# Gate projections with 512 moving columns and one PSUM bank per token block, and one address modulo 512 bytes for all float32r operands

## The chip, the core and the metric

The kernel runs on one core of a Trainium2 chip. A core has a matrix engine (PE, with its weight loads shown as PEld), a vector engine (DVE), an activation engine (ACT), a general engine (POOL) and a queue engine (SP) that issues DMAs. Each takes its own instructions in program order and waits for the others at semaphores. SBUF is the working memory (128 partitions), PSUM the memory that matmuls write to: eight banks of 512 float32 values per partition. The metric is the device time of one execution in microseconds (us); less is better.

## What is computed

One decoder block on 512 tokens of width 1024:

```python
u = rmsnorm(h, norm1_g)
proj = einsum("bsd,de->bse", u, w_in)
(g_qkv, g_z, g_a, g_b, d_q, d_k, d_v, i_q, i_k, i_w, gate_a, gate_b) = split(proj)
...   # gated delta rule on g_qkv, g_a, g_b: o_gdn (8 heads of 128)
o_gdn = rmsnorm(o_gdn, gdn_norm_g) * silu(z)
...   # top-128 sparse attention on d_q, d_k, d_v with the indexer: o_dsa (8 heads of 128)
mixed = sigmoid(gate_a + gb[:D]) * o_gdn + sigmoid(gate_b + gb[D:]) * o_dsa
h = h + mixed @ w_out
hn = rmsnorm(h, norm2_g)
...   # ConvGLU: up 1024 -> 2 x 2816, causal conv of width 3, SiLU gate, down
out = rmsnorm(h, final_g)
```

The change lies in the three projections `g_z`, `gate_a` and `gate_b`, 3 x 1024 columns of `w_in`.

## The kernel before

**Splitting.** Every float32 matrix product is made of three float32r matmuls (`passes`): an operand is split into a rounded part `hi` and a rest `lo`, and `lo*hi`, `hi*lo` and `hi*hi` are added in PSUM. Weights come packed as pieces of 128 x 1024. `piece` loads one into `raw`; ACT rounds it into `whi`, POOL or DVE subtracts it into `wlo`. There are three buffers of each. The normalised tokens stand transposed and split in `uTh`/`uTl`, later in `hTh`/`hTl`.

**Stages, in order of the code.** (1) Input, its norm, the indexer's and the `dv` projections. (2) `gdn_half(0)`: projections of four heads (`channel_major`: weights stationary, 512 tokens moving), convolution and SiLU on DVE and ACT, sums of squares (`kqt`), decay matrices `ge`, Gram matrices (`kk`, into `MT` and `at`), `vt`; then a triangular inverse: blocks of `MT` go through DRAM (`bl`, `nn`) to a loop of 30 pairs of DVE instructions (`tw`, `wi`), back through DRAM into `MT`, then small matmuls (`m`); then a recurrence over four chunks of tokens (`kS`, `TR`, `upd`, `o`). (3) The top-k of the indexer, the `dk` and `dq` projections. (4) `gdn_half(1)`, the same for the other four heads. (5) Attention, 32 items of head and token block (`lg` scores, `pe` softmax, `pT` transposes, `oB`). (6) The gate projections: `token_major` makes 256 columns for 512 tokens, with tokens stationary and weights moving; `z_chunk`, `ga_chunk` and `gb_chunk` apply the results to `at` and `oB`; `mix_chunk` adds both branches and transposes them (`mixT`). (7) Out-projection, (8) up-projection with the ConvGLU, (9) down-projection and the final norm.

**What sets the order.** A scheduler with a timeline of its own merges the stages when the program is built, and fixes a static order of instructions on each engine. Tiles come from pools. A tile with a `tag` takes the next of `bufs` buffers of that tag in the order of the code, and its first writer waits for the last reader of the tile that had the buffer before. PSUM has eight banks under four tags: `acc` 3, `tp` 2, `pT` 1, `rec` 2. All of `kqt`, `kk`, `vt`, `m`, `kS`, `TR`, `upd` and `o` take their bank from `rec`; scores (`lg`) and `mixT` from `tp`; projections from `acc`.

**Places.** A buffer's address follows from the sizes of what was allocated before it. In the built program `whi`, `wlo`, the first tiles of x (`xgh`, `xgl`), `mix` and the first eight `act` tiles begin at byte 448 modulo 512; `uTh`, `uTl`, `hTh` and `hTl` at 128; the other fourteen `act` tiles at 480.

Of the kernel before, what the change touches and what calls it, by code (L numbers as in the profile page):

```python
# [9 lines left out]
F = mybir.dt.float32  # L10
R = mybir.dt.float32r
I32 = mybir.dt.int32
AF = mybir.ActivationFunctionType
OP = mybir.AluOpType
# [7 lines left out]
KT = D // 128  # L22
# [12 lines left out]
    0, 3072, 4096, 4104, 4112, 5136, 5392, 5648, 6160, 6224, 6232, 7256)  # L35


_GATES = [("z", 0), ("z", 1), ("ga", 0), ("ga", 1), ("gb", 0), ("gb", 1), ("gb", 2), ("gb", 3),
          ("z", 2), ("z", 3), ("ga", 2), ("ga", 3)]


def _in_chunks():

    t = []
    t.append(("dv", [_DV, _DV + 128]))
    t.append(("small", None))
    t += [("iq", [_IQ + 256 * j, _IQ + 256 * j + 128]) for j in range(2)]
    gdn = [[("gdn", [_QKV + 1024 * part + 512 * hh + 256 * j + 128 * i for i in range(2)])
            for part in (1, 0, 2) for j in range(2)] for hh in range(2)]
    dsa = [("dk", [_DKV, _DKV + 128])]  # L50
    dsa += [("dq", [_DQ + 256 * j, _DQ + 256 * j + 128]) for j in range(4)]
    t += gdn[0] + dsa + gdn[1]
    off = {"z": _Z, "ga": _GA, "gb": _GB}
    t += [(k, [off[k] + 256 * j, off[k] + 256 * j + 128]) for k, j in _GATES]
    return t


def _pack_weights(w_in, w_out, w_up, w_down):

    out = []  # L60

    def chunk(w, starts):
        c = np.concatenate([w[:, s:s + 128] for s in starts], axis=1)
        c = c.reshape(2, 4, 128, 256).transpose(0, 2, 1, 3).reshape(2, 128, 1024)
        out.extend([c[0], c[1]])

    for kind, starts in _in_chunks():
        if kind == "small":
            c = np.zeros((D, 128), w_in.dtype)
            c[:, 0:64] = w_in[:, _IK:_IK + 64]  # L70
# [12 lines left out]
    return np.ascontiguousarray(np.stack(out))
# [3 lines left out]
def hybrid_block(ctx: ExitStack, tc: tile.TileContext, x: bass.AP, xc: bass.AP, wp: bass.AP,  # L87
                 chan: bass.AP, rows: bass.AP, out: bass.AP):
    nc = tc.nc
    V, A, P, T = nc.vector, nc.scalar, nc.gpsimd, nc.tensor  # L90

    const = ctx.enter_context(tc.tile_pool(name="const", bufs=1))
# [3 lines left out]
    def acc(name="acc"):  # L96
        return psum.tile([128, 512], F, name=name, tag="acc", bufs=3)
# [93 lines left out]
    def piece(lo_engine):  # L191
        raw, hi, lo = load()
        A.copy(hi, raw)  # L193
        lo_engine.tensor_sub(lo, raw, hi.bitcast(F))  # L194
        return hi, lo

    def passes(o, lhs, rhs, first, last, shared=False):


        (lh, ll), (rh, rl) = lhs, rhs  # L200
        a = T.matmul(o, lh, rl, start=first, stop=False, skip_group_check=shared)  # L201
        T.matmul(o, ll, rh, start=False, stop=False, skip_group_check=shared)  # L202
        return a, T.matmul(o, lh, rh, start=False, stop=last, skip_group_check=shared)  # L203

    def cols(pc, k, n, c0, c1):
        return tuple(w.rearrange("p (k c) -> p k c", c=n)[:, k, c0:c1] for w in pc)

    uTh = const.tile([128, KT, S], R, name="uTh", tag="uTh")
    uTl = const.tile([128, KT, S], R, name="uTl", tag="uTl")

# [56 lines left out]
    for tb in range(NT):  # L267
# [3 lines left out]
        _, root = rms_of(ss, out=r4[:, tb:tb + 1])  # L271
# [15 lines left out]
    def u_blk(k, tb):  # L287
        return uTh[:, k, 128 * tb:128 * tb + 128], uTl[:, k, 128 * tb:128 * tb + 128]

    def token_major(eng):  # L290

        pcs = [piece(eng), piece(eng)]
        ps = [acc().rearrange("p (t c) -> p t c", c=256) for _ in range(2)]
        for i in range(2):
            for tb in range(NT):
                for k in range(4):
                    kk = 4 * i + k
                    passes(ps[tb // 2][:, tb % 2], u_blk(kk, tb), cols(pcs[i], k, 256, 0, 256),
                           kk == 0 and tb % 2 == 0, kk == KT - 1, shared=True)
        return ps  # L300

    def channel_major(eng, src=None, second=P):
# [61 lines left out]
    def sc8(name):  # L364
        return const.tile([128, NT, H], F, name=name)
# [1 line left out]
    def b8(ap):  # L367
        return ap.unsqueeze(1).to_broadcast([128, NT, H])

    beta, gd, G, GL, eG, neG, kde, dl = (sc8(n) for n in ("beta", "gd", "G", "GL", "eG", "neG", "kde", "dl"))  # L370
    s0, s1, s2 = sc8("s0"), sc8("s1"), sc8("s2")
    A.activation(beta, sm[:, :, 72:80], AF.Tanh, scale=0.5)
    V.tensor_scalar(beta, beta, 0.5, 0.5, op0=OP.mult, op1=OP.add)
    na = const.tile([128, H], F, name="na")
# [25 lines left out]
    A.activation(dl, GL, AF.Exp)  # L400
    V.tensor_sub(kde, GL, G)
    A.activation(kde, kde, AF.Exp)
    nG = sc8("nG")
    V.tensor_scalar(nG, G, -1.0, None, op0=OP.mult)
    gt = tp("gt")
    T.transpose(gt[0:32, 0:128], G.rearrange("p t h -> p (t h)"), ident)
# [29 lines left out]
    for b in range(1, NT):  # L436
        n = 128 * (b + 1)
        score[b] = mask[:, m_off[b]:m_off[b] + n]
        for h in range(H):
            p = tp("rel")[:, :n]  # L440
# [309 lines left out]
    mix = [[big(FL, "mix") for _ in range(2)] for _ in range(4)]  # L750

    def gate_bias(off):
        gb = PR.tile([128, 256], F, name="gbias", bufs=2)
        A.dma_start(gb, bcast(2048 + off, 256))
        return gb.unsqueeze(1).to_broadcast([128, 2, 256])

    def tmp(name):
        return PR.tile([128, 512], F, name=name, tag="t", bufs=5).rearrange("p (t c) -> p t c", c=256)

    def gated(o, p, bias):  # L760
        t = tmp("tg")
        V.tensor_add(t, p, bias)
        A.activation(t, t, AF.Tanh, scale=0.5)
        V.scalar_tensor_tensor(o, t, 1.0, o, op0=OP.add, op1=OP.mult)

    def z_chunk(j):
        for t2, p in enumerate(token_major(P)):
            t = tmp("tz")
            A.activation(t, p, AF.Tanh, scale=0.5)
            V.scalar_tensor_tensor(t, t, 1.0, p, op0=OP.add, op1=OP.mult)  # L770
            o = oAv[j][:, 2 * t2:2 * t2 + 2]
            P.tensor_mul(o, o, t)

    def ga_chunk(j):
        bias = gate_bias(256 * j)
        for t2, p in enumerate(token_major(P)):
            gated(oAv[j][:, 2 * t2:2 * t2 + 2], p, bias)

    def gb_chunk(j):
        bias = gate_bias(1024 + 256 * j)  # L780
        for t2, p in enumerate(token_major(P)):
            tb = slice(2 * t2, 2 * t2 + 2)
            t = tmp("tg")
            V.tensor_add(t, p, bias)
            A.activation(t, t, AF.Tanh, scale=0.5)
            for i in range(2):
                o = oB[2 * j + i][:, tb]
                V.scalar_tensor_tensor(o, t[:, :, 128 * i:128 * i + 128], 1.0, o, op0=OP.add, op1=OP.mult)

    def mix_chunk(j):  # L790
        for t2 in range(2):
            tb = slice(2 * t2, 2 * t2 + 2)
            pm = tp("mixT").rearrange("p (i t d) -> p i t d", i=2, t=2)
            for i in range(2):
                o = oB[2 * j + i][:, tb]
                V.tensor_add(o, o, oAv[j][:, tb, 128 * i:128 * i + 128])
                for t in range(2):
                    T.transpose(pm[:, i, t], o[:, t], ident)
            ts = slice(256 * t2, 256 * t2 + 256)
            pmv = pm.rearrange("p i t d -> p i (t d)")  # L800
            A.copy(mix[j][0][:, :, ts], pmv)
            V.tensor_sub(mix[j][1][:, :, ts], pmv, mix[j][0][:, :, ts].bitcast(F))

    oAv = [oA[j // 2].rearrange("p t h d -> p t (h d)")[:, :, 256 * (j % 2):256 * (j % 2) + 256] for j in range(4)]
    for kind, j in _GATES:
        {"z": z_chunk, "ga": ga_chunk, "gb": gb_chunk}[kind](j)
        if kind == "gb" and j < 2:
            mix_chunk(j)
        if kind == "ga" and j >= 2:
            mix_chunk(j)  # L810


    hTh = const.tile([128, KT, S], R, name="hTh", tag="uTh")
# [2 lines left out]
    for q in range(2):  # L816
        nc.sync.dma_start(g2b[q], bcast(1024 + 512 * q, 512))
    ss2 = const.tile([128, NT, 4], F, name="ss2")
    load_sqrt(oAv[3][:, 3, 255:256])
    sp2, hns, hg = [], [], []  # L820
    done = None

# [108 lines left out]


    gf = FR.tile([128, D], F, name="gf")
    A.dma_start(gf, bcast(4 * 1024, D))
    sp3 = []
    load_sqrt(act[-1][:, 0, 511:512].bitcast(F))
# [99 lines left out]
```

## Time and profile before

| | us |
|---|---|
| median of 3 runs (lowest, highest) | 971.64 (965.71, 971.94) |
| the profiled execution's own time | 968.83 |
| its span (first to last instruction) | 966.8 |
| PE / DVE / ACT / POOL busy in the span | 932.6 / 614.6 / 439.8 / 206.6 |

The span is what the trace covers; 2.0 us of the execution lie around it. "Busy" of PE joins records that overlap: a matmul's record lasts until its modelled end, long after the next one has begun. What a matmul costs in a dense stretch is therefore the distance from its start to the next start, not its duration.

### The profile page before, as it was taken

To read this page: it belongs to the slowest core of one execution; us is meant where nothing else is said; L and a number is where in the kernel's file an instruction comes from. 1 tells how busy PE (TensorE), PEld (TensorE's weight loads), DVE (VectorE), ACT (ScalarE), POOL (GpSimd) and SP (SyncE) were. 2 spreads that over 40 slices of the span, in tenths; PEclk is the share of its full clock that TensorE was granted. 3 is DMA by queue.
4 is the path that set the end of the run, shared out by engine and by line. 5 is a ranking of instruction groups with operands and counts; after the bars stand their busy time and mean duration, and the time that the engine had idled before them with its cause. 6 is when DMAs were issued, how large, how long until landed. Compare 5 with 4: busy or idle time off the path is not lost.

```text
span 966.8 us, 14652 instructions
## 1 busy us (share of the span) xinstructions
PE 932.6 (96%) x5671; PEld 804.8 (83%) x5671; DVE 614.6 (64%) x1262; ACT 439.8 (45%) x938; POOL 206.6 (21%) x120
## 2 busy tenths in 40 slices
PE   8979999998999998899999999999999999999997
PEld 8768887876887898799999999888888888888886
DVE  5997999997548949754634546655555665522424
ACT  7446674422458762345444435443444443422213
POOL 3734244521201363211343032000000000000201
PEclk9989999997999999999999999999999999999999
DMA  8222222423211131411322222323222323232222
GB/s 326 88 87 87 88 82 72 120 88 88 88 44 44 46 98 66 99 51 50 137 94 93 83 87 89 109 92 104 87 87 97 101 88 105 90 105 92 87 66 87
DMA packets 39541, 89.29 MB, mean 92 GB/s; under 512 B 15632, under 2 KB 16944, under 8 KB 39472
## 3 DMA queue, kind: packets, MB, share of 16 engines
q1 hardware_dynamic: 24048, 82.05, 26.0%
q10 hardware_dynamic: 15424, 6.31, 2.7%
q8 instruction: 44, 0.72, 0.3%
q14 instruction: 25, 0.20, 0.1%
HBM read 85.18 MB, written 3.16 MB: 91 GB/s over the span
## 4 chain that ended last, share of the span: by engine, by line
PE 69%; DVE 23%; DMA 3%; ACT 2%; issue 1%; POOL 1%; ACTq 0%; SPq 0%; DVEq 0%; POOLq 0%
PE acc L201 17%; PE acc L203 17%; PE acc L202 17%; DVE wi L583 3%; PE d L202 3%; PE d L203 3%; PE d L201 3%; DVE mask L687 2%; DVE y L458 2%; DVE top L686 2%; DVE tw L581 2%; PE lg L726 1%; PE lg L708 1%; DVE uv L415 1%; DVE mask L448 1%
## 5 line engine op out<-in xcount | busy, mean ns | idle before, releaser
L193 ACT CAST whi<-raw 128x1024 fp32r<-128x1024 f32 x136 | 142.2, 1046 | 184.9 <-PE acc L203 83.0
L194 POOL TENSOR_TENSOR wlo<-raw,whi 128x1024 fp32r<-128x1024 f32 x60 | 148.8, 2481 | 291.6 <-ACT whi L193 240.1
L194 DVE TENSOR_TENSOR wlo<-raw,whi 128x1024 fp32r<-128x1024 f32 x76 | 94.2, 1240 | 153.5 <-ACT whi L193 153.3
L202 PE MATMUL acc<-hTh,wlo 128*128 128x512 f32 (+1 forms) x368 | 141.7, 385 | 0.0
L201 PE MATMUL acc<-hTl,whi 128*128 128x512 f32 (+1 forms) x368 | 141.1, 386 | 0.2 <-DVE hTl L835 0.2
L203 PE MATMUL acc<-hTh,whi 128*128 128x512 f32 (+1 forms) x368 | 140.8, 385 | 0.0
L201 PE MATMUL acc<-uTl,whi 128*128 128x512 f32 x272 | 110.9, 409 | 6.1 <-DVE iqf L423 5.5
L202 PE MATMUL acc<-uTh,wlo 128*128 128x512 f32 x272 | 110.6, 407 | 1.6 <-DVE wlo L194 1.6
L203 PE MATMUL acc<-whi,uTh 128*128 128x256 f32 x384 | 112.1, 292 | 0.0
L201 PE MATMUL acc<-wlo,uTh 128*128 128x256 f32 x384 | 110.8, 289 | 0.0
L202 PE MATMUL acc<-whi,uTl 128*128 128x256 f32 x384 | 110.8, 289 | 0.0
L203 PE MATMUL acc<-uTh,whi 128*128 128x512 f32 x272 | 110.7, 407 | 0.0
L976 POOL TENSOR_TENSOR h<-h,gf 128x512 f32<-128x512 f32 (+1 forms) x8 | 10.6, 1346 | 346.9 <-ACT sq L972 346.9
L894 DVE SCALAR_TENSOR_TENSOR fy<-acc,ch,fy 128x511 f32<-128x511 f32 x88 | 65.8, 749 | 28.8 <-ACT fy L892 27.0
L201 PEld LDWEIGHTS acc<-hTl,whi 128*128 128x128 f32 x368 | 69.2, 188 | 15.6 <-DVE hTl L835 0.4
L203 PEld LDWEIGHTS acc<-hTh,whi 128*128 128x128 f32 x368 | 69.2, 188 | 15.3
L202 PEld LDWEIGHTS acc<-hTh,wlo 128*128 128x128 f32 x368 | 69.2, 188 | 15.2
L201 PEld LDWEIGHTS acc<-wlo,uTh 128*128 128x128 f32 x384 | 72.8, 190 | 1.6 <-issue 1.0
L203 PEld LDWEIGHTS acc<-whi,uTh 128*128 128x128 f32 x384 | 72.8, 189 | 1.7 <-issue 1.0
L202 PEld LDWEIGHTS acc<-whi,uTl 128*128 128x128 f32 x384 | 72.8, 190 | 1.2 <-issue 1.0
L201 PEld LDWEIGHTS acc<-uTl,whi 128*128 128x128 f32 x272 | 52.4, 193 | 18.6 <-DVE iqf L423 5.9
L202 PEld LDWEIGHTS acc<-uTh,wlo 128*128 128x128 f32 x272 | 52.6, 193 | 13.6 <-DVE wlo L194 2.4
(313 smaller groups left out, 1917.7 us busy)
## 6 DMA issues: line engine op xcount, KB each, us to landing
raw<-in_wp_dram SPq DMA_DIRECT2D x139, 512.0 KB, 3.5
xT<-in_xc_dram SPq DMA_DIRECT2D x8, 256.0 KB, 5.9
xt<-in_x_dram SPq DMA_DIRECT2D x4, 512.0 KB, 7.8
ge<-gdr ACTq DMA_DIRECT2D x8, 256.0 KB, 3.3
h<-in_x_dram SPq DMA_DIRECT2D x4, 512.0 KB, 6.0
out_dram<-h SPq DMA_DIRECT2D x8, 256.0 KB, 2.1
gbias<-in_rows_dram ACTq DMA_DIRECT2D x8, 128.0 KB, 3.4
nn<-bl ACTq DMA_DIRECT2D x4, 256.0 KB, 3.7
```

The source lines that it names most:

```text
L193: A.copy(hi, raw)
L194: lo_engine.tensor_sub(lo, raw, hi.bitcast(F))
L201: a = T.matmul(o, lh, rl, start=first, stop=False, skip_group_check=shared)
L202: T.matmul(o, ll, rh, start=False, stop=False, skip_group_check=shared)
L203: return a, T.matmul(o, lh, rh, start=False, stop=last, skip_group_check=shared)
L458: V.scalar_tensor_tensor(y[:, s:], p[:, :512 - s], cw[:, ti, 3 - s:4 - s], y[:, s:], op0=OP.mult, op1=OP.add)
L581: V.tensor_mul(w, wi[:, 0:c, j:j + 1].to_broadcast([128, c, m]), nn[:, j:j + 1, j + 1:].to_broadcast([128, c, m]))
L583: V.tensor_sub(wi[:, 0:c, j + 1:], wi[:, 0:c, j + 1:], w)
L686: V.max(top, score[b])
L687: V.match_replace(score[b], top, score[b], TAKEN)
L894: V.scalar_tensor_tensor(y[:, s:], p[:, :512 - s], fw[:, ti, 2 - s:3 - s], y[:, s:], op0=OP.mult, op1=OP.add)
L976: P.tensor_mul(hv, hv, gf[:, 512 * half + c.start:512 * half + c.stop])
```

## The change

The gates are made in six chunks of 512 columns in place of twelve of 256. A chunk takes four pieces, each with two blocks of 128 rows of the matrix for all 512 columns; each of the four token blocks has a PSUM bank of its own, the first three from `acc`, the fourth (`tm`) from `rec`. The order of the kinds of gate changes with it, and `mix_chunk` runs for two chunks at a time. The bias of a gate is one tile of 512 in place of two of 256 in turn. Three small pads move the pools so that all operands named under "Places" begin at byte 192 modulo 512; three small tiles share buffers with others to make room (`neG`, `kde`, `nG`).

```diff
-_GATES = [("z", 0), ("z", 1), ("ga", 0), ("ga", 1), ("gb", 0), ("gb", 1), ("gb", 2), ("gb", 3),
-          ("z", 2), ("z", 3), ("ga", 2), ("ga", 3)]
+_GATES = [("z", 0), ("ga", 0), ("gb", 0), ("gb", 1), ("z", 1), ("ga", 1)]
...
-    t += [(k, [off[k] + 256 * j, off[k] + 256 * j + 128]) for k, j in _GATES]
+    t += [(k, [off[k] + 512 * j]) for k, j in _GATES]
...
+        elif len(starts) == 1:
+            c = w_in[:, starts[0]:starts[0] + 512].reshape(4, 2, 128, 512)
+            out.extend(c.transpose(0, 2, 1, 3).reshape(4, 128, 1024))
...
+    pipe.tile([128, 16], F, name="pad1")
...
+    const.tile([128, 16], F, name="pad0")
...
-        pcs = [piece(eng), piece(eng)]
-        ps = [acc().rearrange("p (t c) -> p t c", c=256) for _ in range(2)]
-        for i in range(2):
+        ps = [acc(), acc(), acc(), rec("tm")]
+        for i in range(4):
+            pc = piece(eng)
             for tb in range(NT):
-                for k in range(4):
-                    kk = 4 * i + k
-                    passes(ps[tb // 2][:, tb % 2], u_blk(kk, tb), cols(pcs[i], k, 256, 0, 256),
-                           kk == 0 and tb % 2 == 0, kk == KT - 1, shared=True)
+                for k in range(2):
+                    kk = 2 * i + k
+                    passes(ps[tb], u_blk(kk, tb), cols(pc, k, 512, 0, 512), kk == 0, kk == KT - 1)
...
     def gate_bias(off):
-        gb = PR.tile([128, 256], F, name="gbias", bufs=2)
-        A.dma_start(gb, bcast(2048 + off, 256))
-        return gb.unsqueeze(1).to_broadcast([128, 2, 256])
+        gb = PR.tile([128, 512], F, name="gbias", bufs=1)
+        A.dma_start(gb, bcast(2048 + off, 512))
+        return gb
...
     for kind, j in _GATES:
         {"z": z_chunk, "ga": ga_chunk, "gb": gb_chunk}[kind](j)
-        if kind == "gb" and j < 2:
-            mix_chunk(j)
-        if kind == "ga" and j >= 2:
-            mix_chunk(j)
+        if (kind, j) in (("gb", 0), ("ga", 1)):
+            mix_chunk(2 * j)
+            mix_chunk(2 * j + 1)
...
+    FR.tile([128, 72], F, name="pad2")
```

The static order moves more than the diff shows. On PE, before, at the last `vt` transposes of `gdn_half(1)` (`acc<-wlo,uTh` and the like are gate matmuls, `lg` and `pT` attention):

```order
L201 MATMUL acc<-wlo,uTh 128x256
L202 MATMUL acc<-whi,uTl 128x256
L551 MATMUL vt<-ident,t 128x128 x4
L708 MATMUL lg<-dk,dq 128x384
L203 MATMUL acc<-whi,uTh 128x256
L722 MATMUL pT<-ident,pe 128x128 x2
L201 MATMUL acc<-wlo,uTh 128x256
L551 MATMUL vt<-ident,t 128x128 x4
```

And on PE after the change, at the same place:

```order
L711 MATMUL lg<-dk,dq 128x512
L554 MATMUL vt<-ident,t 128x128 x4
L725 MATMUL pT<-ident,pe 128x128 x3
L554 MATMUL vt<-ident,t 128x128 x12
L729 MATMUL lg<-dv,pT 128x128 x3
L725 MATMUL pT<-ident,pe 128x128 x4
L711 MATMUL lg<-dk,dq 128x128
L729 MATMUL lg<-dv,pT 128x128 x4
```

From the first `vt` to the last `o` of `gdn_half(1)`, 523 gate matmuls stood between its own before; now there is none. Ahead of the last `o` there stood 654 of the 1152 gate matmuls before; now 54 of 576 do, those of the first three pieces for the first three token blocks. On PE after the change, where the recurrence ends, the fourth token block comes in:

```order
L651 MATMUL o<-St,qT 128x128
L652 MATMUL o<-vt,at 128x128
L204 MATMUL tm<-wlo,uTh 128x512
L205 MATMUL tm<-whi,uTl 128x512
L206 MATMUL tm<-whi,uTh 128x512
```

The bank of `tm` is one of the two that the recurrence has used until then, so all that needs it or comes behind it in the three weight buffers stands behind the last `o`. Before, on POOL, at the `ge` and `qT` steps of `gdn_half(1)` and the zeroing of `wi`:

```order
L522 AFFINE_SELECT ge<-ge 128x512
L194 TENSOR_TENSOR wlo<-raw,whi 128x1024
L540 TENSOR_TENSOR qT<-qT,ge 128x4x128
L772 TENSOR_TENSOR at<-at,tz 128x2x256
L540 TENSOR_TENSOR qT<-qT,ge 128x4x128
L522 AFFINE_SELECT ge<-ge 128x512
```

After, on POOL, at that place:

```order
L525 AFFINE_SELECT ge<-ge 128x512
L543 TENSOR_TENSOR qT<-qT,ge 128x4x128
L525 AFFINE_SELECT ge<-ge 128x512
L543 TENSOR_TENSOR qT<-qT,ge 128x4x128 x2
L577 MEMSET wi 64x512
```

The weight splits (`wlo`) and the `z` products have left that place. On DVE, four attention items stood inside the inverse's loop of `gdn_half(1)` and six gate instructions; now nine items stand there and no gate instruction. Behind the last `o` there were seven attention items, now one.

## Rows read from the trace of the kernel before

**Rows 1.** The page: chain of work that ended last, by engine and line.

```profile
PE 69%; DVE 23%; DMA 3%; ACT 2%; issue 1%; POOL 1%; ACTq 0%; SPq 0%; DVEq 0%; POOLq 0%
```

**Rows 2.** Busy time of each engine in two stretches.

```profile
core 0: us, PE busy (x) PEld busy (x) DVE busy (x) ACT busy (x) POOL busy (x), PEclk, DMA share, GB/s
467.60:540.10 72.50, 72.50 (x606) 70.90 (x605) 38.01 (x89) 32.29 (x66) 26.19 (x12) 1.00 0.30 99
588.70:850.00 261.30, 260.96 (x1178) 212.54 (x1177) 152.88 (x192) 112.23 (x148) 5.06 (x3) 1.00 0.29 95
```

**Rows 3.** Gate matmuls: count, duration, first and last start.

```profile
L203 PE MATMUL acc<-whi,uTh x384: 276/279/682, 321.1 to 540.0; 128*128 128x256 f32 x192
```

**Rows 4.** Last `o` of either half on PE (start us, us).

```profile
295.79 0.39 PE L649 MATMUL o<-vt,at 128*128 128x128 f32 x2
...
467.39 0.39 PE L649 MATMUL o<-vt,at 128*128 128x128 f32 x2
```

**Rows 5.** Gate matmuls in a dense stretch, nine starts apart.

```profile
526.88 0.28 PE L201 MATMUL acc<-wlo,uTh 128*128 128x256 f32 x1
...
527.93 0.28 PE L201 MATMUL acc<-wlo,uTh 128*128 128x256 f32 x1
```

**Rows 6.** Moving x (448) on stationary weights (448), 17 starts apart.

```profile
20.96 0.39 PE L201 MATMUL acc<-xgl,whi 128*128 128x512 f32 x1
...
24.81 0.39 PE L203 MATMUL acc<-xgh,whi 128*128 128x512 f32 x1
```

**Rows 7.** Up-projection, moving `hT` (128) on weights (448), 14 starts apart.

```profile
699.81 0.40 PE L201 MATMUL acc<-hTl,whi 128*128 128x512 f32 x1
...
703.08 0.40 PE L203 MATMUL acc<-hTh,whi 128*128 128x512 f32 x1
```

**Rows 8.** Down-projection, stationary late `act` (480), moving weights (448), 13 starts apart.

```profile
880.03 0.40 PE L202 MATMUL acc<-whi,act 128*128 128x512 f32 x1
...
883.07 0.40 PE L203 MATMUL acc<-whi,act 128*128 128x512 f32 x1
```

**Rows 9.** The chain in `gdn_half(1)`, and the first `TR` of either half.

```profile
263.64 0.89 PE TR L638 x8
...
357.23 3.40 DMA nn<-bl
360.72 1.54 DVE wi L576
...
393.12 0.50 DVE UT L591
393.69 2.96 DMA bl<-wi
...
401.58 1.93 DVE at L764
...
423.76 0.89 PE TR L638 x8
```

**Rows 10.** POOL and DVE at one moment of the loop.

```profile
377.48 2.38 POOL L194 TENSOR_TENSOR wlo<-raw,whi 128x1024 fp32r<-128x1024 f32 x1 [4.46 <-ACT whi L193]
377.53 2.47 DVE L583 TENSOR_TENSOR wi<-wi,tw 128x120 f32<-128x120 f32 x1
```

**Rows 11.** DVE by group inside the loop, 360.6 to 393.2 us.

```profile
L583 DVE TENSOR_TENSOR wi<-wi,tw 128x110 f32<-128x110 f32 (+20 forms) x30 | 14.6, 487 | 0.7
L581 DVE TENSOR_TENSOR tw<-wi,nn 128x110 f32<-128x110 f32 (+20 forms) x30 | 8.4, 281 | 0.6
L711 DVE TENSOR_TENSOR pe<-lg,mask 128x512 f32<-128x512 f32 (+3 forms) x4 | 1.9, 482 | 0.0
L764 DVE SCALAR_TENSOR_TENSOR at<-tg,at 128x512 f32<-128x512 f32 x2 | 1.4, 688 | 0.0
```

**Rows 12.** PE's clock after a stretch with little PE work.

```profile
225.00:228.00 3.00, 0.27 (x2) 0.00 (x0) 0.50 (x1) 0.68 (x2) 0.00 (x0) 0.95 0.44 77
228.00:238.00 10.00, 9.74 (x81) 7.58 (x82) 8.96 (x12) 3.73 (x6) 2.37 (x1) 0.50 0.22 61
```

More of the change, by code (lines that the diff above doesn't have):

```diff
@@ L368, in b8 @@
         return ap.unsqueeze(1).to_broadcast([128, NT, H])
-    beta, gd, G, GL, eG, neG, kde, dl = (sc8(n) for n in ("beta", "gd", "G", "GL", "eG", "neG", "kde", "dl"))
+    beta, gd, G, GL, eG, dl = (sc8(n) for n in ("beta", "gd", "G", "GL", "eG", "dl"))
     s0, s1, s2 = sc8("s0"), sc8("s1"), sc8("s2")
+    neG, kde, nG = s0, s2, s1
     A.activation(beta, sm[:, :, 72:80], AF.Tanh, scale=0.5)
@@ L402, in hybrid_block @@
     A.activation(kde, kde, AF.Exp)
-    nG = sc8("nG")
     V.tensor_scalar(nG, G, -1.0, None, op0=OP.mult)
@@ L752, in gate_bias, with half_gate @@
     def gate_bias(off):
-        gb = PR.tile([128, 256], F, name="gbias", bufs=2)
-        A.dma_start(gb, bcast(2048 + off, 256))
-        return gb.unsqueeze(1).to_broadcast([128, 2, 256])
+        gb = PR.tile([128, 512], F, name="gbias", bufs=1)
+        A.dma_start(gb, bcast(2048 + off, 512))
+        return gb
     def tmp(name):
-        return PR.tile([128, 512], F, name=name, tag="t", bufs=5).rearrange("p (t c) -> p t c", c=256)
-    def gated(o, p, bias):
+        return PR.tile([128, 512], F, name=name, tag="t", bufs=5)
+    def half_gate(p, bias):
         t = tmp("tg")
@@ L763, in gated @@
         A.activation(t, t, AF.Tanh, scale=0.5)
-        V.scalar_tensor_tensor(o, t, 1.0, o, op0=OP.add, op1=OP.mult)
+        return t
     def z_chunk(j):
-        for t2, p in enumerate(token_major(P)):
+        for tb, p in enumerate(token_major(P)):
             t = tmp("tz")
@@ L770, in z_chunk @@
             V.scalar_tensor_tensor(t, t, 1.0, p, op0=OP.add, op1=OP.mult)
-            o = oAv[j][:, 2 * t2:2 * t2 + 2]
-            P.tensor_mul(o, o, t)
+            P.tensor_mul(oAv[j][:, tb], oAv[j][:, tb], t)
     def ga_chunk(j):
-        bias = gate_bias(256 * j)
-        for t2, p in enumerate(token_major(P)):
-            gated(oAv[j][:, 2 * t2:2 * t2 + 2], p, bias)
+        bias = gate_bias(512 * j)
+        for tb, p in enumerate(token_major(P)):
+            t = half_gate(p, bias)
+            V.scalar_tensor_tensor(oAv[j][:, tb], t, 1.0, oAv[j][:, tb], op0=OP.add, op1=OP.mult)
     def gb_chunk(j):
[L780 to L788, printed above, removed]
+        bias = gate_bias(1024 + 512 * j)
+        for tb, p in enumerate(token_major(P)):
+            t = half_gate(p, bias)
+            for i in range(4):
+                o = oB[4 * j + i][:, tb]
+                V.scalar_tensor_tensor(o, t[:, 128 * i:128 * i + 128], 1.0, o, op0=OP.add, op1=OP.mult)
     def mix_chunk(j):
@@ L795, in mix_chunk @@
                 o = oB[2 * j + i][:, tb]
-                V.tensor_add(o, o, oAv[j][:, tb, 128 * i:128 * i + 128])
+                c = 256 * (j % 2) + 128 * i
+                V.tensor_add(o, o, oAv[j // 2][:, tb, c:c + 128])
                 for t in range(2):
@@ L802, in mix_chunk @@
             V.tensor_sub(mix[j][1][:, :, ts], pmv, mix[j][0][:, :, ts].bitcast(F))
-    oAv = [oA[j // 2].rearrange("p t h d -> p t (h d)")[:, :, 256 * (j % 2):256 * (j % 2) + 256] for j in range(4)]
+    oAv = [o.rearrange("p t h d -> p t (h d)") for o in oA]
     for kind, j in _GATES:
         {"z": z_chunk, "ga": ga_chunk, "gb": gb_chunk}[kind](j)
-        if kind == "gb" and j < 2:
-            mix_chunk(j)
-        if kind == "ga" and j >= 2:
-            mix_chunk(j)
+        if (kind, j) in (("gb", 0), ("ga", 1)):
+            mix_chunk(2 * j)
+            mix_chunk(2 * j + 1)
     hTh = const.tile([128, KT, S], R, name="hTh", tag="uTh")
@@ L818, in hybrid_block @@
     ss2 = const.tile([128, NT, 4], F, name="ss2")
-    load_sqrt(oAv[3][:, 3, 255:256])
+    load_sqrt(oAv[1][:, 3, 511:512])
     sp2, hns, hg = [], [], []
```

## Prediction

> **What bounds the kernel now.** I began with the chain of waits on the page: 69% of it is PE and 23% DVE [rows 1]. The chain in order of time puts the DVE share into the first 230 us and into the inverse of `gdn_half(1)`; from about 400 us it is PE almost alone. The windows by stage agree: from 467.6 us on PE is never idle [rows 2]. Next I read where the gate matmuls lie. They run from 321 to 540 us [rows 3], while `gdn_half(1)` goes through its inverse and its recurrence, whose last `o` is at 467.4 [rows 4]. They are the work with which PE fills a long chain of other engines. So one gate matmul more or less is worth its price only if PE would have something else to do at that moment.
>
> **The change, part by part.**
>
> *Price of a gate matmul.* Records overlap, so starts are what counts. Gates with 256 columns come (527.93 - 526.88)/9 = 0.1167 us apart [rows 5]. For 512 columns there are two prices. Moving x on weights, both at byte 448 modulo 512, gives (24.81 - 20.96)/17 = 0.2265 [rows 6]; moving `hT` at 128 on weights at 448 gives (703.08 - 699.81)/14 = 0.2336 [rows 7]; `act` at 480 under weights at 448 gives 3.04/13 = 0.2338 [rows 8]. The shape is the same, and the cheap rows are those with equal places. I take 0.2265 for every 512-column matmul after the change. 1152 gates at 0.1167 are 134.4 us, 576 at 0.2265 are 130.5: the gates alone give 4 us.
>
> *The places elsewhere.* 336 x 3 = 1008 up-projection matmuls save 0.0071 each, 7.2 us; 98 x 3 = 294 of the down-projection on late `act` save 0.0073, 2.1 us. PE is dense there [rows 2], so these 9 us shorten the end. 816 projections on `uT` become cheaper as well, 5.8 us in all, but most lie in the first 230 us, where the chain is DVE's; I count nothing for them, and 2 us at most. If the place is not what sets the two prices, the 9 us go.
>
> *The order.* This is the large term. A chunk now needs a bank of `rec` for its fourth token block. The recurrence takes all its banks from the two of `rec`, so in the static order the first `tm` stands behind its last `o`. The other three blocks can't go on alone, because a piece of weights is free only when all four blocks have used it, and there are three weight buffers. Ahead of the last `o` stand 54 gate matmuls (12 us of PE) where 654 (76 us) stood. PE has only attention and the half's own small matmuls left to do there, and the remaining gates come in one block behind it.
>
> *How much of that is covered?* The time t of the last `o` sets it. Before, it is 467.4 + 0.4 = 467.8 [rows 4].
> - Start of the loop: the last `ge` select on POOL is no longer queued behind a weight split of 2.4 us (the length as in [rows 10]). 360.7 [rows 9] becomes 358.3.
> - The loop, 360.7 to 393.1 = 32.4 us [rows 9]. When POOL does a split or a product with `at`, a DVE instruction that begins at that moment lasts until POOL is done: 2.47 us in place of about 0.25 [rows 10]. The 60 instructions are 14.6 + 8.4 = 23.0 us [rows 11]; at 0.25 they would be 15, so 8 us are such stalls, and POOL has no work there now. Six gate instructions (0.69 each [rows 11], 4 us) leave; five more attention items come in, two passes of 0.48 [rows 11] and some 0.3 us of small ones each, 6 us. 32.4 - 8 - 4 + 6 = 26.4: the loop ends at 384.7.
> - From there to the first `TR`: 423.8 - 393.1 = 30.7 us before [rows 9]. Two DRAM passages are in it and remain. A gate product of 1.93 us stood ahead of the inverse's copies, with two more of 0.7, and gate matmuls stood between the small ones; I take off 8 and add 3 for a PE clock that falls in the gap (below): 25.7, so `TR` at 410.4.
> - The recurrence: 467.8 - 423.8 = 44 us in this half, but 296.2 - 263.6 = 32.6 in `gdn_half(0)`, where projections stood among its first chunk only [rows 4, 9]. With attention alone beside it I take 29.
>
> That gives t = 439.5, 28 us earlier. With nothing gained but the loop's start t would be 465; with the loop at 21, the passage at 20 and the recurrence at 23 it would be 422.
>
> *What follows the last `o`.* Before: 540.1 - 467.8 = 72.3 us [rows 3, 4], for 498 gates (58 us), seven attention items, 24 transposes `mixT`. Now: 522 gates x 0.2265 = 118.2; one item and 16 transposes, some 4; and about 2 until the fourth piece, whose buffer waits for the first `tm` matmuls, is split. 124 us: the gates end at 439.5 + 124 = 563.5, where they ended at 540.1. That is 23.4 us later.
>
> *With one answer.* The single bias tile waits for the chunk before, but its DMA has three quarters of a chunk (16 us) until the first use. Two `mix` chunks at the end, not one, leave a tail of some 1 us under the first out-projection pieces. The pads and the shared small tiles cost nothing that a row shows.
>
> *The sum.* 966.8 + 23.4 - 9.3 + 1 = 982 us of span, and 2.0 around it: **984 us**, against 968.8 for the profiled execution. The median of the runs shown is 2.8 above that execution; I put the forecast between the two, at 986.
>
> [...]
>
> **The rivals.**
> 1. *The chain runs much faster than I think once the gates are out of its way* (the other side: faster). The place is 358 to 440 us. The price is 1 us of the end for each us of t. It decides at t = 425, below which the change gains, and a gain of over 1% needs t = 415 or less: 358.3 + 20 (loop) + 18 + 19. For it: POOL's stalls and gate products do leave DVE. Against it: nine attention items come into the loop, and 19 us for the recurrence is less than half of what this half took and 13 less than the other half. At t = 422 to 430 the time is 967 to 976; at 413 it is 958.
> 2. *The gates' halved count is a gain by itself*: 4 us of gates and 9 of places, and PE stays filled, 956. The order speaks against it: no gate matmul stands between `vt` and the last `o`. It would need the attention to fill PE, and 19 items of about 1.4 us are 27 us in 90.
> [...]
> 4. *The places do nothing*: 9 to 11 us more than the forecast, 996.
>
> **How the numbers follow.** Forecast, t between 430 and 450, 976 to 997 us: 0.60. Rival 1: 0.17, of it 0.05 with a gain of over 1%. Rival 2: 0.03. Rival 3: 0.14. Rival 4: 0.06. About 1% (10 us) is what a measurement of this kernel can tell from no change. Slower by more than 981 us: most of the forecast (0.46) and rivals 3 and 4, 0.66. Faster than 962: 0.08. Within: 0.26. The range that leaves out 2 in 10 runs from 968, a t of 422, to 1004, a t of 458.
>
> **What would show it.** In the new trace: a stretch from about 350 to 440 us in which PE's start-to-start work is about half, where it was filled; the first `tm` right behind the last `o`, near 440; gate matmuls about 0.2265 apart and ending near 563; up-projection starts 0.2265 apart, not 0.2336; `wi` instructions without the 2.4 us stalls. The prediction is wrong if gate matmuls stand among the recurrence, if the last `o` is before 425 or after 455, or if the up-projection's spacing does not move.

## The result, and the profile after

The changed kernel takes **992.5 us** in the median of four runs (989.5 to 993.7), the kernel before 968.7 in four beside it: a ratio of 1.0236, 95% interval 1.0208 to 1.0264. It is slower, as forecast (986; range 968 to 1004). The profiled execution took 989.5 us, its span is 987.8.

The page of the changed kernel, its chain of work by engine and the slices of PE's clock (against [rows 1]):

```profile
PEclk9989999998999986699999999999999999999999
...
PE 65%; DVE 24%; ACT 5%; DMA 3%; issue 1%; ACTq 1%; POOL 0%; SPq 0%; DVEq 0%; POOLq 0%
```

The two slices with a 6 are 370 to 420 us. The stretches around them, by windows (for [rows 2] and [rows 12]):

```profile
core 0: us, PE busy (x) PEld busy (x) DVE busy (x) ACT busy (x) POOL busy (x), PEclk, DMA share, GB/s
...
361.20:392.30 31.10, 21.64 (x67) 14.13 (x68) 21.63 (x96) 10.79 (x33) 0.00 (x0) 0.62 0.00 1
392.30:415.60 23.30, 19.99 (x268) 15.26 (x267) 11.72 (x25) 6.37 (x17) 0.00 (x0) 0.63 0.15 25
415.60:440.40 24.80, 24.38 (x191) 22.54 (x190) 14.51 (x48) 18.46 (x68) 0.00 (x0) 1.00 0.00 1
440.40:568.20 127.80, 124.83 (x568) 102.44 (x567) 55.46 (x108) 44.70 (x69) 60.70 (x29) 1.00 0.37 122
617.80:850.00 232.20, 231.95 (x1077) 194.01 (x1076) 140.71 (x177) 101.40 (x134) 4.96 (x3) 1.00 0.30 98
```

The rows are the inverse's loop, the way from there to the first `TR`, the recurrence, the gates behind it, and the up-projection. POOL has nothing to do in the first three, PE has 67 matmuls in 31 us of the first, at a mean granted clock of 0.62 (windows of 4 to 6 us within it show from 0.50, at 366 to 371, to 0.93, at 372.2 to 376.2), and from 440 us PE is nearly full again (124.83 of 127.80 us). PE around the last `o`, in order of time (start us, us), answers [rows 4]:

```profile
440.03 0.39 PE L652 MATMUL o<-vt,at 128*128 128x128 f32 x2
440.17 0.47 PE L204 MATMUL tm<-wlo,uTh 128*128 128x512 f32 x1
```

The first `tm` comes 0.14 us behind it. The gates by bank, with first and last start (for [rows 3]), and the first stage's projections:

```profile
L206 PE MATMUL tm<-whi,uTh x48: 387/389/481, 440.7 to 568.0; 128*128 128x512 f32 x48
...
L206 PE MATMUL acc<-whi,uTh x144: 387/389/481, 324.9 to 566.7; 128*128 128x512 f32 x144
...
L204 PE MATMUL acc<-uTl,whi x272: 387/389/796, 48.0 to 323.0; 128*128 128x512 f32 x136
```

The gates end at 568, 28 us later than before. Starts in dense stretches, for [rows 5], [rows 7] and [rows 8]: 24, 11 and 14 apart.

```profile
458.09 0.39 PE L206 MATMUL tm<-whi,uTh 128*128 128x512 f32 x1
...
463.53 0.39 PE L206 MATMUL tm<-whi,uTh 128*128 128x512 f32 x1
...
699.63 0.39 PE L206 MATMUL acc<-hTh,whi 128*128 128x512 f32 x1
...
702.12 0.39 PE L205 MATMUL acc<-hTh,wlo 128*128 128x512 f32 x1
...
899.77 0.39 PE L204 MATMUL acc<-wlo,act 128*128 128x512 f32 x1
...
902.95 0.39 PE L206 MATMUL d<-whi,act 128*128 128x512 f32 x1
```

That is 0.2267, 0.2264 and 0.2271 us from one start to the next: one price for all three, as the forecast had it. The chain in order of time, for [rows 9]:

```profile
357.12 4.04 DMA nn<-bl
...
366.09 1.66 PE lg L711 x2
367.77 0.56 DVE pe L714
...
392.26 0.48 DVE UT L594
...
415.64 0.89 PE TR L641 x8
```

In the middle stands what was not there before: DVE in the loop, waiting for `lg` of the attention (in the loop before, DVE had no such wait). DVE's waits in the loop (us in total, times, longest), and its groups there (busy us, mean ns, idle before; for [rows 10, 11]):

```profile
DVE pe L714 <- PE lg L711: 8.1, 7, 2.2
...
L584 DVE TENSOR_TENSOR tw<-wi,nn 128x110 f32<-128x110 f32 (+20 forms) x30 | 7.4, 246 | 1.0 <-DMA nn<-bl 0.5
L586 DVE TENSOR_TENSOR wi<-wi,tw 128x110 f32<-128x110 f32 (+20 forms) x30 | 7.3, 244 | 0.4
L714 DVE TENSOR_TENSOR pe<-lg,mask 128x128 f32<-128x128 f32 (+3 forms) x9 | 4.2, 468 | 8.1 <-PE lg L711 8.1
```

The loop's own 60 instructions fell from 23.0 [rows 11] to 14.7 us: POOL's stalls are gone, 8.3 us where the forecast had 8. But nine items are in the loop, and DVE takes their `pe` in the order written out for it, also when `lg` isn't there: 8.1 us of waiting took the place of 8.3 us of stalls.

### The profile page after: what moved, and what is told of

Read it like the earlier page. It is cut to its first block, busy times and chain, and to the rows that moved or that the text cites. A ratio compares the mean times of both kernels' runs of the same rounds, so it can differ in the third digit from the quotient of the medians.

```text
span 987.8 us, 13528 instructions
## 1 busy us (share of the span) xinstructions
PE 936.6 (95%) x5095; PEld 784.5 (79%) x5095; DVE 612.4 (62%) x1278; ACT 439.5 (44%) x938; POOL 206.2 (21%) x120
## 4 chain that ended last, share of the span: by engine, by line
PE 65%; DVE 24%; ACT 5%; DMA 3%; issue 1%; ACTq 1%; POOL 0%; SPq 0%; DVEq 0%; POOLq 0%
PE acc L204 15%; PE acc L206 15%; PE acc L205 15%; DVE y L461 3%; PE d L205 3%; PE d L206 3%; PE d L204 3%; DVE mask L690 2%; PE lg L711 2%; DVE top L689 2%; PE lg L729 1%; DVE wi L586 1%; DVE at L675 1%; DVE tw L584 1%; DVE mask L451 1%
## 5 line engine op out<-in xcount | busy, mean ns | idle before, releaser
L204 PE MATMUL acc<-hTl,whi 128*128 128x512 f32 (+1 forms) x368 | 139.1, 381 | 0.2 <-DVE hTl L835 0.2
L206 PE MATMUL acc<-hTh,whi 128*128 128x512 f32 (+1 forms) x368 | 138.8, 380 | 0.0
L206 PEld LDWEIGHTS acc<-uTh,whi 128*128 128x128 f32 x272 | 52.4, 193 | 10.4
L204 PE MATMUL acc<-wlo,uTh 128*128 128x512 f32 x144 | 56.8, 394 | 0.6 <-DVE tz L773 0.5
L461 DVE SCALAR_TENSOR_TENSOR y<-acc,cw,y 128x511 f32<-128x511 f32 (+2 forms) x72 | 52.6, 739 | 7.7 <-ACT y L459 7.0
L205 PE MATMUL acc<-whi,uTl 128*128 128x512 f32 x144 | 56.2, 390 | 0.0
L206 PE MATMUL acc<-whi,uTh 128*128 128x512 f32 x144 | 55.9, 390 | 0.0
L892 ACT ACTIVATE fy<-acc,ch 128x512 f32<-128x512 f32 x44 | 34.2, 778 | 36.8 <-PE acc L206 36.6
```

The costliest lines, as they stand in the source:

```text
L461: V.scalar_tensor_tensor(y[:, s:], p[:, :512 - s], cw[:, ti, 3 - s:4 - s], y[:, s:], op0=OP.mult, op1=OP.add)
L892: A.activation(y, p, AF.Identity, scale=fw[:, ti, 2:3], bias=fb[:, ti:ti + 1])
```

## The experiments

All times are medians, and each ratio is to the kernel before, run beside it. The places in the program, from each profiled execution (us; the loop starts with the first `wi` and ends at `UT`; in the changed kernel and in e5 the first `wi` came 1 us earlier, at 360.2 and 365.5, and the start given is where the second `nn` transfer has landed):

| kernel | loop starts | ends | first `TR` | last `o` done | gates end | span | time | ratio |
|---|---|---|---|---|---|---|---|---|
| before | 360.7 | 393.1 | 423.8 | 467.8 | 540.1 | 966.8 | 968.7 | |
| after | 361.2 | 392.3 | 415.6 | 440.4 | 568.2 | 987.8 | 992.5 | 1.024 |
| e1, places alone | 363.9 | 396.0 | 426.7 | 471.2 | 544.8 | 963.5 | 964.8 | 0.996 |
| e2, gates alone | 365.1 | 397.3 | 420.8 | 445.8 | 574.5 | 1002.2 | 1004.7 | 1.037 |
| e3, bank alone | 358.8 | 385.9 | 413.3 | 439.9 | 575.5 | 1002.2 | 1003.8 | 1.037 |
| e4, two chunks early | 363.0 | 398.6 | 434.9 | 460.2 | 549.1 | 991.7 | 992.0 | 1.025 |
| e5, no attention | 366.4 | 383.5 | 406.0 | 430.8 | 556.9 | 976.5 | 978.6 | 1.012 |
| e7, one chunk early | 363.1 | 395.6 | 420.2 | 445.6 | 560.1 | 979.7 | 980.0 | 1.012 |
| e8, two bias loads | 361.3 | 389.1 | 418.4 | 444.4 | 573.2 | 992.7 | 994.3 | 1.028 |
| e9, two places | 361.5 | 393.7 | 424.2 | 468.4 | 540.7 | 959.3 | 960.0 | 0.992 |
| e10, PE kept busy | 362.8 | 381.9 | 411.8 | 439.5 | 574.9 | 994.5 | 996.0 | 1.025 |

### The bank alone (e3), and the gates alone (e2)

```diff
 # e3, in the kernel before
-        ps = [acc().rearrange("p (t c) -> p t c", c=256) for _ in range(2)]
+        ps = [q.rearrange("p (t c) -> p t c", c=256) for q in (acc(), rec("tm"))]
 # e2, in the changed kernel: pad0, pad1, pad2 and the line that shares s0, s1, s2 are out
-    neG, kde, nG = s0, s2, s1
```

> The kernel before with one word changed: the second bank of a gate chunk is taken from rec, not from acc. Chunks stay at 256 columns, 12 of them, and the places are those of before. Theory (the bank's tag alone moves the gates): the gates pile up behind the last o, which comes near 440, not 467; some 1000 gates by 0.117 behind it end near 565, 25 us later than before, and the time is 988 to 998 us. Rival (the width of the chunk is what costs, by its four blocks that wait for each piece of weights): the time stays at 966 to 972.

> The changed kernel without the pads and the shared tiles: gates of 512 columns with a bank of rec, operands at their old places (uT at 128, weights at 448, late act at 480 modulo 512). Theory: what the places gave goes back, 9.3 us of up- and down-projection and 576 gates by 0.0071, 4 us: 992.5 + 13 = 1003 to 1008 us; the first tm stays behind the last o, near 440. Rival (the places do nothing): 990 to 994. A second rival (the two halves of the change need each other, since the pads shift the order): any time under 985.

e3 took 1003.8 us, 1.0366 times before (1.0349 to 1.0382); e2 1004.7, 1.0368 (1.0340 to 1.0396). e3 around its last `o`, and the gates of its `tm` (first and last start):

```profile
439.55 0.39 PE L649 MATMUL o<-vt,at 128*128 128x128 f32 x2
439.69 0.36 PE L201 MATMUL tm<-wlo,uTh 128*128 128x256 f32 x1
...
L203 PE MATMUL tm<-whi,uTh x192: 278/279/573, 440.0 to 575.4; 128*128 128x256 f32 x192
```

One word, with chunks and places as before, moves the last `o` to 439.9 and costs 35 us. The end is 10 us later than expected: 1080 gates stand behind the `o`, not 1000, and 136 us with the attention between them; so the time is 6 us above its range. e2 hit its range. Between e3 and e2 only the width differs (with the order of the kinds of gate, the bias tile and the static order that follow from it): 1 us. So the rival that width costs falls. The 4 us that the forecast gave to the gates don't show in e2 either. Gates 24 starts apart in e2:

```profile
499.90 0.39 PE L203 MATMUL tm<-wlo,uTh 128*128 128x512 f32 x1
...
505.39 0.39 PE L203 MATMUL tm<-wlo,uTh 128*128 128x512 f32 x1
```

That is 0.2288 us. 576 gates at this price are 131.8 us, 2.6 less than 1152 at 0.1167, and only 1.2 more than at the 0.2267 of the changed kernel, where e2's expectation had 4. The stretch behind the `o` is shorter in e2 than in e3 (128.7 and 135.6 us), but mostly since more of the work stands ahead of it: 54 wide gates are 12 us, e3's 72 narrow ones 8. And the last `o` is 6 us later in e2, with the first gate at 327.8 (320.6 in e3). So e2's range was hit partly by luck: against the changed kernel 8.1 us of its span lie behind the gates, as expected of the places, but 5.4 in the time of the last `o`, which the expectation left near 440, and 0.9 between.

### The places alone (e1), and two places (e9)

```diff
 # e1: the kernel before with pad0, pad1, pad2 and
+    neG, kde, nG = s0, s2, s1
 # e9: e1 without pad0, uT and hT in one tile, hT 64 bytes on; pad1 and pad2 resized
+        t = const.tile([128, 2 * KT * S + 16], R, name="uT", tag="uT")
+        t = t[:, o:o + 2 * KT * S].rearrange("p (a k s) -> p a k s", a=2, s=S)
...
+    uTh, uTl = two_places(0)
...
+    hTh, hTl = two_places(16)
```

> The kernel before with the three pads and the shared small tiles only; the gates stay as they were (12 chunks of 256 columns, banks of acc alone), and all float32r operands stand at byte 192 modulo 512. Theory (the place sets the price, and the loss of the whole change is the gates' order): up-projection starts 0.2265 apart in place of 0.2336, 7.2 us, late act 2.1 us, at most 2 us from uT: 957 to 960 us, against 968.7. The order of the gates is that of before, the last o stays near 467. Rival (the place does nothing, and the cheaper starts in the changed kernel have another cause): 968 to 970, with starts 0.2336 apart.

e1 took 964.8 us, 0.9959 (0.9945 to 0.9973): faster, but by 4 us and not by 9, so neither side had it. The first and the last `hTl` matmul of its up-projection start 241.9 us apart, as in the changed kernel with its 0.2267 (before: 248.2), as expected, and the stretch behind the gates is 8 us shorter. The gates, though, end 4.7 us later. What goes the other way is in their rows, e1 and then e9 (min, median and max ns), and in e1's starts, 20 apart:

```profile
L204 PE MATMUL acc<-whi,uTh x384: 277/283/682, 322.9 to 544.7; 128*128 128x256 f32 x192
...
524.19 0.28 PE L202 MATMUL acc<-wlo,uTh 128*128 128x256 f32 x1
...
526.58 0.28 PE L204 MATMUL acc<-whi,uTh 128*128 128x256 f32 x1
```

```profile
L204 PE MATMUL acc<-whi,uT x384: 276/279/681, 321.6 to 540.6; 128*128 128x256 f32 x192
```

A gate of 256 columns had a median of 279 ns before [rows 3] and has 283 at equal places; its starts go from 0.1167 [rows 5] to (526.58 - 524.19)/20 = 0.1195. For this shape the equal place is the dearer of these two. e9 was made to test that.

> The kernel with the places alone, but uT 320 bytes away from the weights modulo 512, as in the kernel before, and hT, in the same tile from 64 bytes on, 256 away from them; late act and weights at one place. The gates are those of before, 12 chunks of 256 columns. Theory (512-column matmuls get cheaper at equal places, 0.2336 to 0.2265, but 256-column ones dearer, 0.117 to 0.120, and 1152 gates by 0.003 are why the places alone gave 3.6 us and not 9): gates at 0.117 again, up-projection at 0.2265, 959 to 963 us. Rival (the missing 5 us went somewhere else): 964 to 966.

e9 took 960.0 us, 0.9922 (0.9898 to 0.9945), inside its range, with the gates back at 279 ns. From the first gate to the end of the gates it takes 219 us, as before, where e1 takes 222: 3 of e1's 4.7 us were the gates' price. The other 2 us lie ahead of e1's first gate (322.6, before 320.8, e9 321.3), and no run shows why. e9 beats both kernels. No wide gates are in it.

### Which places are equal (e6)

```diff
 # in the changed kernel
-    pipe.tile([128, 16], F, name="pad1")
+    pipe.tile([128, 80], F, name="pad1")
...
-    FR.tile([128, 72], F, name="pad2")
+    FR.tile([128, 24], F, name="pad2")
```

> The changed kernel with other pads: uT and hT at byte 192 under weights at 448 modulo 512 (256 apart), late act at 384 under weights at 448 (64 apart); in the kernel before these were 320 and 32 apart. Theory (equal places modulo 512 are what counts): hT and late act starts go back to 0.231 to 0.236 us, gates too, and the time is 1003 to 1008 us. Rival A (equal modulo 256 is enough): hT and gates stay at 0.2265, late act at 0.2336, 994 to 996 us. Rival B (equal modulo 64 is enough): all stay at 0.2265, 990 to 994.

One run, 991.7 us. Starts in its up-projection (10 apart) and on late `act` (14 apart):

```profile
699.72 0.39 PE L206 MATMUL acc<-hTh,whi 128*128 128x512 f32 x1
...
701.98 0.39 PE L204 MATMUL acc<-hTl,whi 128*128 128x512 f32 x1
...
902.76 0.39 PE L204 MATMUL acc<-wlo,act 128*128 128x512 f32 x1
...
905.97 0.39 PE L206 MATMUL d<-whi,act 128*128 128x512 f32 x1
```

0.226 for operands 256 bytes apart, 0.2293 for 64 apart, so the theory falls. By price the nearest is rival A, equal modulo 256 is enough, but for late `act` it had 0.2336; the time can't tell A from B, as 294 matmuls by 0.0028 are 0.8 us.

### Gates into the gap (e4, e7)

```diff
 # in gdn_half(hh), between vt and the inverse; 1 in place of 2 in e7
+        if hh:
+            for kind, j in _GATES[:2]:
+                {"z": z_chunk, "ga": ga_chunk}[kind](j)
...
-    for kind, j in _GATES:
+    for kind, j in _GATES[2:]:
```

> The changed kernel with the same six chunks of 512 columns, the same banks and places, but the first two chunks (z 0 and ga 0) are written into gdn_half(1) between vt and the inverse, so that they ask for their banks of rec ahead of the inverse's and the recurrence's. Theory (the place in the order of rec is the whole loss): 192 gates, 43.5 us of PE, move into 350 to 400 us, where PE stood idle or at the lower clock; the last o comes 5 to 15 us later than 440 because POOL's splits and the gate products are back beside the loop; the gates end at 538 to 548 in place of 568, and the time is 960 to 973 us, less than before's 968.7 or level with it. Rival (512-column chunks cost by themselves, by stalls on four blocks and on bank turnover): 985 or more.

> As the kernel with two chunks written into gdn_half(1), but with one (z 0). Theory: 96 gates, 21.7 us of PE, move into the stretch beside the inverse, and the gates' end comes some 20 us earlier, less what the last o is late: 970 to 978 us, half way between the changed kernel and the one with two chunks. Rival (each chunk in the loop delays the recurrence by as much as it fills): 988 to 995.

e7 took 980.0 us (1.0119, 1.0096 to 1.0143), 12 less than the changed kernel, 2 us above its range. e4 took 992.0 (1.0246, 1.0220 to 1.0273): its expectation failed and the time is the rival's, though the last `o` (460) and the gates' end (549) are only 5 and 1 us later than it had them. So the loss is not the rival's stalls in the gates; it comes behind them. Windows of e4 behind its last `o`, columns as above, and its `lg` (last start):

```profile
460.00:549.00 89.00, 87.97 (x420) 72.32 (x419) 47.67 (x117) 36.93 (x76) 39.69 (x17) 1.00 0.31 106
549.00:565.00 16.00, 8.87 (x35) 5.79 (x33) 11.10 (x28) 7.65 (x18) 0.00 (x0) 0.68 0.12 42
...
L763 PE MATMUL lg<-dv,pT x160: 270/275/582, 284.3 to 570.1; 128*128 128x128 f32 x160
```

The attention, which ends at 473 in the changed kernel, ends at 570 in e4 (537 in e7): the early chunks took its place in the gap, and in e4 PE is out of gates at 549 and waits for the last items, at a granted clock of 0.68. What fills the gap pushes out what filled it.

### The attention left out (e5)

```diff
-    pipe.tile([128, 16], F, name="pad1")
+    pipe.tile([128, 40], F, name="pad1")
...
-    items = [(h, b) for h in range(H) for b in range(NT)]
-    st = attend_a(*items[0])
-    for i, it in enumerate(items):
...
+    for h in range(H):
+        oB.append(half_kb("oB").rearrange("p (b d) -> p b d", d=128))
+        V.memset(oB[h], 0.0)
```

> The changed kernel with the attention's 32 items left out (its outputs are set to zero by DVE; dq, dk and the scores are still computed). Theory (in the loop of the inverse DVE waits 8 us for lg, in the order written out for it, and that is why the loop did not get faster): the loop, from the nn transfer to UT, takes 20 to 24 us instead of 31, the small matmuls of the inverse and the recurrence meet no attention ahead of them, and the last o comes at 418 to 428; the gates follow it at once and the time is 965 to 978 us. Rival (the loop is bound by its own 60 instructions and the passages): the loop stays at 29 to 31 us, the last o at 436 to 440, the time at 980 or more, since only the few us of attention behind the o are saved.

e5, which leaves the attention out, took 978.6 us (1.0118, 1.0094 to 1.0142), just above its range. The chain of e5, and one row of the changed kernel's:

```profile
362.34 4.06 DMA nn<-bl
...
383.52 0.50 DVE UT L594
...
399.32 3.32 PE m L619 x29
...
406.00 2.02 PE TR L641 x8
```

```profile
409.84 2.08 PE m L619 x32
```

The loop takes 17.1 us, less than expected, and the last `o` comes at 430.8, not 418 to 428: PE has no matmul in the loop, its granted clock is 0.50 there and from 383.5 to 406 us, and `m` takes 3.3 us for 29 where the changed kernel has 2.08 for 32, at a granted clock of 0.97. That the loop is 14 us shorter without the attention is shown; that the `o` could come at 425 or less is not.

### Two bias loads (e8), and PE kept busy (e10)

```diff
 # e8
-        A.dma_start(gb, bcast(2048 + off, 512))
+        for c in (0, 256):
+            A.dma_start(gb[:, c:c + 256], bcast(2048 + off + c, 256))
 # e10, ahead of the loop and in it
+        if hh:
+            wd = rec("wd")
...
+            if hh:
+                T.transpose(wd[0:c, 0:128], wi[:, 0:c, j], ident)
+                for _ in range(5):
+                    T.transpose(wd[:, 0:128], ident, ident)
```

> The changed kernel with one edit: each bias of 512 columns is loaded by two transfers of 256, in place of one. The kernel before issues two bias transfers on ACT near 50 us, the changed one issues one, and from that row on the static order of all engines in the first 320 us is another one; with two transfers it is that of the kernel before again. Theory (the other order costs the first stage 6 us: from the first uT projection to the first gate matmul 276.7 us in place of 270.7): the stage goes back to 270 to 271, the last o comes some 5 us earlier, and the time is 984 to 989 us. Rival (the stage's length follows the places or the start of the program, not the order): 991 to 994, the stage at 276.

The first stage went back, 50.3 to 319.3 us for the row that had 48.0 to 323.0, as the theory had it; the time did not: 994.3 us (1.0276, 1.0255 to 1.0296), 0.3 above the rival's range, and the last `o` came 4 us later, not 5 earlier. So the theory had the stage and the rival, within a little, the time. The loop starts at 361.3, no earlier than in the changed kernel. One bias transfer more or less, for a bias that DVE first reads at 475 us, does change the static order of the first stage, and the 6 us there did not reach the time.

> The changed kernel with 180 small transposes of no use on PE, six behind each of the 30 steps of the inverse's loop in gdn_half(1), in a bank of rec that is free there. They cost PE some 20 us at the higher clock, in a stretch where it has 31. Theory (in the loop DVE waits 8 us for lg because PE runs at the lower clock): the granted clock of the loop goes from 0.62 to 0.9 or more, an lg pair of 384 columns takes 0.7 us in place of 1.7, DVE's waits for lg fall from 8 to 3 us or less, the loop takes 24 to 27 us, the last o comes at 432 to 436 and the time is 984 to 989 us. Rival (DVE waits because the attention's own chain is long and stands in its order, at any clock): the clock rises, but the waits stay at 6 to 10 us, the loop at 30 or more, and the time at 991 to 1000.

996.0 us (ratio 1.0246, 1.0177 to 1.0315; three runs at 996, one at 985.7, so the median can't tell it from the changed kernel). Windows of the loop, the way to `TR`, the recurrence and the gates behind it, columns as above:

```profile
362.80:381.90 19.10, 18.56 (x168) 17.91 (x169) 16.45 (x71) 1.73 (x6) 0.00 (x0) 1.00 0.01 2
381.90:411.80 29.90, 26.58 (x295) 21.66 (x293) 12.19 (x27) 7.06 (x19) 0.00 (x0) 0.61 0.12 19
411.80:439.50 27.70, 27.06 (x193) 24.41 (x193) 14.40 (x45) 19.63 (x68) 0.00 (x0) 0.93 0.14 51
439.50:575.00 135.50, 133.68 (x628) 110.13 (x627) 55.73 (x136) 53.11 (x93) 63.94 (x29) 1.00 0.30 105
```

The granted clock of the loop rose to 1.00 and the loop fell to 19.1, but the order changed with it: two items stand in the loop, not nine. The others stand behind it, the way to `TR` is 6.6 us longer at 0.61, the gates' stretch 7.7 us longer, and the last `o` is at the same place. DVE's waits for `lg` in the loop and behind it, to 411.8 (us in total, times, longest):

```profile
DVE pe L720 <- PE lg L717: 0.2, 1, 0.2
...
DVE pe L720 <- PE lg L717: 10.5, 3, 5.5
```

The waits have moved with the items, out of the loop, and have not become fewer. How much of the 8.1 us in the changed kernel is the clock and how much the chain of an item stays open, as clock and order changed together.

## Why the prediction was right, step by step

**The order** was the large term, and it is shown: the bank's tag alone (e3) moves the gates and costs 35 us. All 522 gates and the first `tm` were where the forecast had them.

**The time of the last `o`**, forecast 439.5, was 440.4, but that it came within 1 us is luck: its four steps were off by +2.9, +4.7, -2.4 and -4.2 us, and cancelled.
- The loop's start, 358.3: it was 361.2. In e3, where the first stage stands in the old order, it is 358.8, which the argument from POOL's queue gave. That the order of the first stage would change too was not in the forecast; but in e8, whose first stage is as short as before, the loop starts at 361.3 as well, so what holds it back in the changed kernel stays open.
- The loop, 26.4: it was 31.1. This is the term that was mis-sized. The stalls (8) were right: 23.0 became 14.7. In the loop before, five of the 60 began within 0.4 us of the start of a POOL instruction and ended within 0.14 us of its end, 1.28 to 2.47 us long; the other 55 took 0.18 to 0.29. In the changed kernel POOL has no instruction there. The items were counted by their DVE work, 6 us, without the waits for `lg` (8.1). In e3, with seven items and 3.4 us of such waits, the loop took 27.0.
- To `TR`, 25.7: it was 23.3, 7.4 less than before, at a mean granted clock of 0.63 where it was 1.00 before. No run shows the 3 us that the forecast has there for the clock: what the absent gate work gained and what the clock cost are not told apart. The recurrence, 29: it was 24.8, with PE at 1.00 and nothing but attention between. With attention beside it and lower mean clocks it was 26.0 (e8, 0.95), 26.6 (e3, 0.97) and 27.7 (e10, 0.93); without the attention, at 0.86, it was 24.8 (e5). How much is the clock and how much the attention stays open.

**Behind the `o`**, 124: it was 127.8. PE stood idle for 3.0 of the difference, at these places in order of time (in brackets: idle before, and for whom):

```profile
456.16 0.50 PE L204 MATMUL acc<-wlo,uTh 128*128 128x512 f32 x1 [0.52 <-DVE tz L773]
...
466.37 0.66 PE L725 MATMUL pT<-ident,pe 128*128 128x128 f32 x4 [2.45 <-ACT pe L717]
```

The attention's last item comes late, since DVE is held up just then by the end of `gdn_half(1)` (16 products into `at`, 7.5 us from 456.0). The forecast had PE dense.

**The places elsewhere**, -9.3 and a tail of +1: from the gates' end to the end of the span it was 426.7 us [rows 3] and is 419.6, so -7.1; the tail (gates' end to the first up-projection) grew by 0.9, and the rest fell by 8.0, from 378.0 to 370.0. Of the 1.3 that lack, 0.6 are the 96 up-projection matmuls of 256 columns, whose starts went from (592.43 - 588.79)/32 = 0.114 to (621.63 - 617.79)/32 = 0.120 apart. The rest is the shortness of the rows: over all dense starts of the up-projection the mean went from 0.2333 to 0.2267, a gain of 0.0066 and not 0.0071, and on late `act` it gained some 0.0063 and not 0.0073, 0.8 us together. That the pads cost nothing was wrong for the kernel with narrow gates (e1 against e9); for this one no run shows a cost.

**With one answer** (the single bias tile): DVE never waits for the bias in the gates' stretch, as forecast.

In sum: 28.1 us later at the gates' end (forecast 23.4), 7.1 back (8.3), 21.0 of span (forecast 15). The profiled execution took 989.5 us where the sum had 984: the mechanism was right and the size 5.5 us short.

**The rivals.** The first needs the last `o` at 415 to 425; no kernel here has it, not even the one without attention (430.8). Its loop of 20 us can be had (17.1 in e5, 19.1 in e10), its 18 to `TR` and its 19 for the recurrence in no run. The second fell with the order. For the 0.14 of rival 3: the mean granted clock was 0.62 in the loop, 0.63 behind it and 1.00 in the recurrence, and the last `o` came at 440.4. Windows of the changed kernel, columns as above:

```profile
400.00:410.00 10.00, 10.00 (x175) 6.88 (x175) 6.38 (x15) 2.89 (x8) 0.00 (x0) 0.50 0.01 3
410.00:420.00 10.00, 10.00 (x114) 9.67 (x114) 4.53 (x12) 5.39 (x15) 0.00 (x0) 1.00 0.01 2
```

From 400 us PE is busy without a gap, with the small matmuls of the inverse and attention, at a mean granted clock of 0.50 to 410 and of 1.00 from there. What sets the granted clock no run shows: in e10's loop it was 1.00 with PE busy for 18.56 of 19.10 us, and here it was 0.50 with 10.00 of 10.00. The fourth fell: the spacing moved with the places in e1 (gates 0.1167 to 0.1195 us), in e6 (late `act` 0.2271 to 0.2293) and in e9 (a gate's median 279 ns, 283 in e1), where nothing else was changed but three shared small tiles, and e2, which differs from the changed kernel in the places, is 8.1 us longer behind the gates.

## What to carry to other kernels

Before you give a step one more bank, look which tag has it, and who asks for that tag ahead of it: work that fills another chain's gaps must not ask for anything that the chain holds. When such work leaves, count what comes into its place by its waits too; when it is moved back, expect it to push out what has taken its place: in eight kernels here with the gates behind the `o`, or part of them moved ahead of it again, the time went from 980 to 1005, and none came to 968. Price a matmul by shape and place together, from rows of that shape.

## What was not expected of the hardware

The same float32r matmul shape stood at several spacings in dense stretches, from 0.226 to 0.2338 us for 512 columns and from 0.114 to 0.120 for 256, by where its operands lie. Between places 0 and 320 bytes apart, 512 columns were cheaper at 0 and 256 columns at 320. The table has what was measured; "bytes apart" is the distance between the start addresses of the stationary and the moving operand, taken modulo 512 as in the forecast. That 512 is the right measure, or what other distances cost, is not shown.

| columns, moving operand | bytes apart: us from start to start |
|---|---|
| 512, tokens | 0: 0.2265 [rows 6]; 256: 0.226 (e6); 320: 0.2336 [rows 7] |
| 512, weights | 0: 0.2267 (changed kernel); 64: 0.2293 (e6); 320: 0.2288 (e2); 32: 0.2338 [rows 8] |
| 256, weights (gates) | 0: 0.1195 (e1); 320: 0.1167 [rows 5] |
| 256, tokens (`hT`) | 0: 0.120 (changed kernel); 320: 0.114 (before) |

So for 512 columns, 320 bytes apart were 0.007 us dearer than 0 with the tokens moving and 0.002 with the weights moving. Why is not shown by any run. e9 takes the cheaper of the measured places for the gates and for the 512 columns of the up- and down-projection (not for the projections on `uT`): 0.8% of the kernel's time, by moving tiles and sharing three small ones.
